# Two gate groups taken into an eighth set of block products, and a fixed pattern of partner steps

## The chip, the cores and the metric

The kernel runs on one NeuronCore of a Trainium2 chip. The metric is device time in microseconds (us) of one execution. Three runs of the kernel before gave 1090.18, 1089.87 and 1087.65 us, a median of 1089.87 us. The engines are named as in the profile: PE (TensorE, the matrix engine), PEld (its weight loads), DVE (VectorE), ACT (ScalarE), POOL (GpSimd) and SP (SyncE, which only issues transfers here).

## What is computed

One decoder layer on 256 tokens of width 2048. A single projection `h @ w_in` makes all inputs of two token mixers; each mixer is normed, gated by a SiLU, projected, and both are merged by sigmoid gates and projected out:

```python
proj = h @ w_in[l]
(a_q, a_k, a_v, a_g, a_lr, b_q, b_k, b_v, b_g, m_a, m_b) = jnp.split(proj, offsets, axis=-1)
...
o_a = rmsnorm(o_a, gla_norm_g[l]).reshape(B, S, GLA_VAL_DIM) * jax.nn.silu(a_g)
y_a = o_a @ w_branch_a[l]
...
o_b = o_b.reshape(B, S, DIFF_VAL_DIM) * jax.nn.silu(b_g)
y_b = o_b @ w_branch_b[l]
merged = jax.nn.sigmoid(m_a) * y_a + jax.nn.sigmoid(m_b) * y_b
out = merged @ w_out[l]
```

`o_a` is a gated linear attention (4 heads, called GLA below), `o_b` a differential attention (16 heads in four groups of four, each with queries `dq` and keys `dk`). Everything is in fp32. The columns of `a_g`, the gate of GLA, come in four groups of 512, called `ag0` to `ag3`; `m02`, `m03` are groups of `m_a`.

## The kernel before

**Three products for one.** A weight tile of 128 x 1024 numbers (a *half*) is loaded from HBM, rounded by ACT to a high part `hi` (L357), and the remainder `lo = w - hi` is made by DVE (L358). Each matmul product is then hi x hi, hi x lo, lo x hi, so a half is used by three matmuls per 128 x 512 block. `emit_half` prepares halves in the order of a list, `take` hands them to PE; `AHEAD` is 3, and there are three `hi` and three `lo` buffers, so preparation runs at most three halves ahead of PE.

**Plain products.** `token_major` computes a group of 512 columns for all 256 tokens in eight halves of 12 matmuls. `channel_major` (and `half_channel`, L552 is the shared `mm` helper) computes 128 columns with channels on partitions, two halves of 16 matmuls each: eight with 512 columns and eight with 256.

**Block products.** In the *phase*, sets of 1024 columns are computed by seven block products instead of eight (a fast 2 x 2 block scheme; `PRODUCTS` gives the order 1, 3, 5, 6, 2, 7, 4). Of the weight blocks the kernel needs sums, and builds them in two *chains* `a` and `b` (four buffers of 128 x 2048 in all, each chain in two parts t = 0 and 1):

- `link` loads a block into a chain; the POOL queue issues it (L227) once the buffer is free. The buffer of `a` part 0 of the next set is the one that product 7 part 0 frees; the last two are freed by product 4.
- After product 1 has been prepared, `follow_set` issues, for each half, a transfer that *accumulates* another block onto `a` (POOL queue, L251, 512 KB each, four per set). Product 5 reads the result.
- At steps (5,1), (6,0), (2,1) and (7,0) DVE adds `b` or the block `c` onto `a` (L260, two adds each); after the first two of these a block is accumulated onto `b` by a transfer, for product 7.

A *step* below is one slot (product, part): two halves of six matmuls. One set has 14 such slots. The last, smaller set (a *quarter* set, `SETS`) has only part 0 of each product: it gives the first half of the sum over channels for `ag3` and `m02`, whose other half is done plainly later.

**Partner steps.** Between slots, `phase_steps` puts halves of plain products (`v4`, GLA's keys and queries, `dq`/`dk` of the head groups in `EARLY`): the partners. Their weights are loaded by SP's queue (L308, 1 MB for the two halves of one channel tile, three `raw` buffers), so they need no chain. The phase's PE order is pinned as the list says.

Before, there are seven full sets, and each slot has one partner except 21 slots in `skip`: in sets 1 to 6 these are (4,0), (2,0) and (1,0), and (4,1) too in sets 5 and 6. So a set has 11 partners (10 at the end), 88 in all with four more at the start of set 0. The quarter set has six.

**After the phase** come `ag0` to `ag3` (`token_major`, then tanh on ACT and a gate on DVE, in `gate`), `m02`, the head group 3 (`diff_heads`), `m03`, and then the branch projections. Between their halves `pump` issues pieces of the GLA scores (exponentials, products and masks on ACT and DVE, small matmuls in `bg` banks), later GLA's output and the attention heads. Results of the phase wait in HBM (`spill`, POOL queue) and are fetched again.

Of the kernel before, what the change touches and what calls it, by code (L numbers as in the profile page):

```python
# [10 lines left out]
AF = mybir.ActivationFunctionType  # L11
# [3 lines left out]
P = 128  # L15
# [11 lines left out]
ROWS = {"two": 2, "tok": 4, "chan": KT}  # L27
WARM = 10
PRODUCTS = (1, 3, 5, 6, 2, 7, 4)
SETS = 7  # L30
QUARTER = ("ag3", "m02")
MERGE = (0, 1, 6)
LEAD = 6
EARLY = (0, 1, 2)
BIG = 18
MORE = 16
BRIDGE = 512
# [12 lines left out]
def chunk_plan():  # L50

    plan = [("v0", "two", "w_in", [(6144, RANK), (2048, 2 * VG[0] - RANK)])]
    at = 2 * VG[0] - RANK
    for g, n in enumerate(VG[2:]):
        plan.append((f"v{g + 2}", "tok", "w_in", [(2048 + at, n)]))
        at += n
    for hf in range(2):
        for name, base in (("k", 1024), ("q", 0)):
            for c in range(4):
                plan.append((f"{name}{hf}{c}", "chan", "w_in", [(base + 512 * hf + P * c, P)]))  # L60
    o = 6144 + RANK
    for s in range(2):
        plan.append((f"set{s}", "set", "w_in", [(o + 10240 + 1024 * s, 1024)]))
    for s in range(2, 6):
        plan.append((f"set{s}", "set", "w_in", [(o + base + 512 * (s - 2), 512) for base in (4096, 6144)]))
    plan.append(("set6", "set", "w_in", [(o + 8192, 1024)]))
    plan.append((f"set{SETS}", "quarter", "w_in", [(5632, 512), (o + 9216, 512)]))
    for g in range(4):
        plan.append((f"ag{g}", "rest" if g == 3 else "tok", "w_in", [(4096 + 512 * g, 512)]))
        for c in range(4):  # L70
            for n, name in enumerate(("dq", "dk")):
                plan.append((f"{name}{g}{c}", "chan", "w_in", [(o + 2048 * n + 512 * g + P * c, P)]))
        if g > 1:
            plan.append((f"m0{g}", "rest" if g == 2 else "tok", "w_in", [(o + 8192 + 512 * g, 512)]))
        for br in range(2):
            kind = "late" if br and g < 2 else "tok"
            plan.append((f"y{br}{g}", kind, ("w_branch_a", "w_branch_b")[br], [(512 * g, 512)]))
        plan.append((f"o{g}", "late", "w_out", [(512 * g, 512)]))
    plan.append(("ys0", "half", "w_branch_b", [(c, 512) for c in BRANCH_COLS]))
    for s, cols in enumerate(LATE_COLS):  # L80
        plan.append((f"os{s}", "half", "w_out", [(c, 512) for c in cols]))
    return plan
# [17 lines left out]
def phase_steps():  # L100

    keys = ["v4"] + [f"{name}{hf}{c}" for hf in range(2) for name in ("k", "q") for c in range(4)]
    keys += [f"{name}{g}{c}" for g in EARLY for pair in range(2) for name in ("dq", "dk") for c in (2 * pair, 2 * pair + 1)]
    other = [(key, r, h) for key in keys for r in range(4 if key == "v4" else 1) for h in range(2)]
    slots = [(s, prod, t) for s in range(SETS) for prod in PRODUCTS for t in range(2)]
    slots += [(SETS, prod, 0) for prod in PRODUCTS]
    front = [(0, prod, t) for prod in PRODUCTS[:2] for t in range(2)]
    skip = [(SETS, 4, 0), (SETS - 1, 4, 1), (SETS - 2, 4, 1)] + [(s, prod, 0) for prod in (4, 2, 1) for s in range(SETS - 1, 0, -1)]
    skip = skip[: len(slots) + len(front) - len(other)]
    mixed = []  # L110
    for slot in slots:
        mixed += [("set", *slot, h) for h in range(2)]
        for _ in range((slot not in skip) + (slot in front)):
            mixed.append(other.pop(0))
    return mixed + other

# [27 lines left out]
def hybrid_kernel(ctx: ExitStack, tc, xt, xn, preg, postg, w, w2, gkb, glag, lamv, diffg, ident_d, causal_d, lmask_d, out):  # L144
# [61 lines left out]
        return halves_of(*(f"{name}{g}{c}" for pair in range(2) for name in ("dq", "dk") for c in (2 * pair, 2 * pair + 1)))  # L206

    seq = halves_of("v0", "v2", "v3") + phase_steps()
    seq += halves_of(*(f"ag{g}" for g in range(4)))
    seq += halves_of("m02") + heads_order(3) + halves_of("m03", *(f"y0{g}" for g in range(4)))[:-4]  # L210
    seq += branch_steps() + late_steps() + halves_of("o2", "o3")
    ready = {}
    emitted = [0]
# [613 lines left out]
    def block_products(s):  # L827
        x = ps("mm")
        bank = {1: x, 6: x, 7: x, 4: x}
        kept, halves = {}, {}  # L830

        def right_done(b):
            dst = halves["r"][:, b, :]
            if s == SETS:
                return
            if s in MERGE:
                act.activation(dst, dst, AF.Tanh, scale=minus_half[:, b : b + 1])
            else:
                t = t2([P, 512], "tanh")
                act.activation(t, dst, AF.Tanh, scale=half_rstd[:, b : b + 1])  # L840
                dve.scalar_tensor_tensor(out=dst, in0=t, scalar=-1.0, in1=dst, op0=ALU.add, op1=ALU.mult)

        def left_done(b, src):
            if s in MERGE:
                act.activation(halves["l"][:, b, :], src, AF.Tanh, scale=half_rstd[:, b : b + 1])
            elif s < SETS:
                act.activation(halves["l"][:, b, :], src, AF.Copy, scale=rstd[:, b : b + 1])
            elif b:
                act.activation(halves["l"][:, b, :], src, AF.Copy)

        for prod in PRODUCTS:
            if prod not in bank:
                bank[prod] = ps("mm")
            out = bank[prod]
            few = 1 if s == SETS else 2
            for t in range(few):
                for h in range(2):
                    hi, lo = take(("set", s, prod, t, h))
                    for w, parts in ((hi, (0, 1)), (lo, (0,))):
                        for j in range(2):  # L860
                            kt = 4 * t + 2 * h + j
                            a = operand(prod, kt)
                            for part in parts:
                                first = prod not in (6, 7, 4) and kt == 0 and w is hi and part == 0
                                last = kt == 4 * few - 1 and w is lo
                                i = mm(out, a[part], w[:, 512 * j : 512 * j + 512], start=first, stop=last, skip_group_check=out is x)
                    latest[0] = i.ins
                    if t == few - 1 and h:
                        if prod in (1, 5):
                            kept[prod] = t2([P, 512], f"p{prod}")  # L870
                            act.activation(kept[prod], out, AF.Copy)
                        if prod == 5:
                            kept[3] = t2([P, 512], "p35")
                            dve.tensor_tensor(out=kept[3], in0=bank[3], in1=kept[5], op=ALU.add)
                        if prod == 6:
                            halves["r"] = u([P, 2, 512], "gr")
                            with tc.high_priority(offset=100):
                                dve.tensor_tensor(out=halves["r"][:, 0, :], in0=x, in1=kept[3], op=ALU.add)
                            right_done(0)
                        if prod == 2:  # L880
                            halves["l"] = u([P, 2, 512], "gl")
                            dve.tensor_tensor(out=halves["l"][:, 0, :], in0=out, in1=kept[1], op=ALU.add)
                            left_done(0, halves["l"][:, 0, :])
                        if prod == 7:
                            with tc.high_priority(offset=100):
                                dve.tensor_tensor(out=halves["r"][:, 1, :], in0=x, in1=kept[5], op=ALU.add)
                            right_done(1)
                            gspill[2 * s + 1] = spill(halves["r"], "gr")
                        if prod == 4:
                            left_done(1, x)  # L890
                            gspill[2 * s] = spill(halves["l"], "gl")
                    yield
# [376 lines left out]
    def other_parts(n):  # L1269
        return [fetch(gspill[n][:, b, :], "rest", lambda shape, name, dtype: t2(shape, name)) for b in range(2)]  # L1270

    for g in range(4):
        parts = other_parts(2 * SETS) if g == 3 else None
        banks = token_major(f"ag{g}", 512, x_ops, LANES)
        t = u2([P, 2, 512], "ua")
        for b in range(2):
            src = banks[b]
            if parts:
                src = parts[b]
                dve.tensor_tensor(out=src, in0=banks[b], in1=src, op=ALU.add)  # L1280
            gate(src, b, t[:, b, :])
        gates.append(t)
# [19 lines left out]
    m0.extend(gspill[12:14])  # L1302
    parts = other_parts(2 * SETS + 1)
    merge_gate(token_major("m02", 512, x_ops, LANES), parts)
    diff_heads(3)
    merge_gate(token_major("m03", 512, x_ops, LANES))

    while "out" not in done:
# [361 lines left out]
```

## Time and profile before

| | us |
|---|---|
| three runs | 1090.18, 1089.87, 1087.65 |
| median | 1089.87 |
| span of the profiled execution | 1087.3 |
| DVE busy in the span | 930.8 |
| ACT busy in the span | 720.0 |
| DMA traffic | 288.21 MB, mean 265 GB/s |

The span runs from the first to the last instruction of the profiled execution; the page gives no other time of that execution, and the median of the runs is 2.6 us above its span. "Busy" is the time in which an engine had an instruction under way, and a busy PE isn't one at its peak. DVE instructions follow each other before the one ahead has fully ended, so a run of them is read from start to start. A DMA row "to landing" is the time from issue to the last byte.

### The profile page before, as it was taken

What the parts mean: (1) busy time and instruction counts of PE and PEld (TensorE: products, weight loads), DVE (VectorE), ACT (ScalarE), POOL (GpSimd) and SP (SyncE); (2) the same over time, 40 slices, a digit from 0 to 9 for tenths busy, and PEclk for the clock granted to TensorE, in tenths of its full rate; (3) what the DMA queues carried; (4) which work ended last, traced back from release to release, by engine and by line L of the source; (5) the groups of instructions that cost most, each with busy time, mean ns of one, the idle gap of its engine ahead of it and who ended that gap; (6) DMA issues with size and microseconds to landing.
All of it is one profiled execution on the core that took longest, in us unless ns stands there. A gap on an engine that the chain in (4) does not pass through costs nothing.

```text
span 1087.3 us, 15367 instructions
## 1 busy us (share of the span) xinstructions
PE 1079.5 (99%) x5440; PEld 925.4 (85%) x5440; DVE 930.8 (86%) x1295; ACT 720.0 (66%) x1047; POOL 154.5 (14%) x229
## 2 busy tenths in 40 slices
PE   9999999999999999999999999999999999999997
PEld 8999888888888888888888888888888888888886
DVE  7787987979979899798998899877778878889886
ACT  7886766676766767667676465556777767566662
POOL 0201112121121211212102100021011011100000
PEclk9999999999999999999999999999999999999999
DMA  9889869799797997979968656599898898988752
GB/s 351 286 296 331 241 252 295 210 354 224 258 272 213 364 243 269 295 190 365 241 242 248 239 181 208 180 326 324 259 297 258 280 298 261 333 293 264 272 187 104
DMA packets 64941, 288.21 MB, mean 265 GB/s; under 512 B 8480, under 2 KB 11552, under 8 KB 46944
## 3 DMA queue, kind: packets, MB, share of 16 engines
q1 hardware_dynamic: 39520, 183.72, 48.2%
q0 software_dynamic: 24768, 102.77, 34.6%
q8 instruction: 43, 0.70, 0.3%
q10 hardware_dynamic: 576, 0.73, 0.2%
q14 instruction: 34, 0.28, 0.1%
HBM read 260.98 MB, written 26.21 MB: 264 GB/s over the span
## 4 chain that ended last, share of the span: by engine, by line
PE 88%; issue 5%; DMA 4%; DVE 2%; POOL 1%; ACT 0%; POOLq 0%; ACTq 0%; DVEq 0%
PE mm L552 54%; PE bg L552 24%; DMA a<-in_w_dram 2%; PE mm L540 2%; PE bg L540 2%; PE mm L525 1%; PE bg L977 1%; DVE lo L358 1%; DMA b<-in_w_dram 1%; PE bg L525 1%; DMA dl<-dk 1%; PE bg L1145 0%; PE bg L1119 0%; PE bg L444 0%; PE bg L1120 0%
## 5 line engine op out<-in xcount | busy, mean ns | idle before, releaser
L357 ACT ACTIVATE hi<-raw 128x1024 fp32r<-128x1024 f32 (+3 forms) x253 | 259.2, 1031 | 185.8 <-PE bg L552 89.9
L358 DVE TENSOR_TENSOR lo<-raw,hi 128x1024 fp32r<-128x1024 f32 (+3 forms) x255 | 300.3, 1183 | 63.9 <-ACT hi L357 59.3
L552 PE MATMUL mm<-hi,xs 128*128 128x512 f32 (+1 forms) x808 | 204.3, 386 | 0.0
L552 PEld LDWEIGHTS mm<-hi,xs 128*128 128x128 f32 x808 | 149.7, 188 | 25.0 <-ACT hi L357 0.2
L358 DVE TENSOR_TENSOR lo<-a,hi 128x1024 fp32r<-128x1024 f32 x120 | 144.7, 1220 | 23.7 <-ACT hi L357 22.9
L552 PE MATMUL bg<-xs,hi 128*128 128x512 f32 x640 | 164.9, 389 | 0.0
L357 ACT ACTIVATE hi<-a 128x1024 fp32r<-128x1024 f32 x120 | 127.0, 1060 | 47.2 <-PE mm L552 27.4
L552 PEld LDWEIGHTS bg<-xs,hi 128*128 128x128 f32 x640 | 120.3, 188 | 23.4
L552 PE MATMUL mm<-lo,xs 128*128 128x512 f32 (+1 forms) x404 | 113.1, 384 | 0.3 <-DVE lo L358 0.2
L552 PEld LDWEIGHTS bg<-xs,lo 128*128 128x128 f32 x640 | 87.2, 190 | 6.3
L552 PE MATMUL bg<-xs,lo 128*128 128x256 f32 x640 | 89.2, 282 | 0.0
L552 PEld LDWEIGHTS mm<-lo,xs 128*128 128x128 f32 x404 | 75.5, 188 | 14.6 <-DVE lo L358 1.1
L358 DVE TENSOR_TENSOR lo<-b,hi 128x1024 fp32r<-128x1024 f32 x60 | 72.4, 1221 | 6.5 <-ACT hi L357 5.0
L357 ACT ACTIVATE hi<-b 128x1024 fp32r<-128x1024 f32 x60 | 63.5, 1061 | 17.0 <-PE mm L552 14.7
L552 PE MATMUL mm<-hi,oah 128*128 128x512 f32 x128 | 50.8, 397 | 0.0
L552 PE MATMUL mm<-hi,oal 128*128 128x512 f32 x128 | 50.0, 391 | 0.0
L251 POOL DMA_DIRECT2D b<-in_w_dram x30 | 26.0, 869 | 138.5 <-DVE a L260 112.1
L1131 ACT ACTIVATE prob<-prob,mx,score_scale 128x128 f32<-128x128 f32 x64 | 34.3, 539 | 8.2 <-DVE mx L1126 8.0
L552 PE MATMUL mm<-hi,obh 128*128 128x512 f32 x96 | 37.7, 393 | 0.0
L552 PE MATMUL mm<-hi,obl 128*128 128x512 f32 x96 | 37.4, 390 | 0.0
L260 DVE TENSOR_TENSOR a<-a,b 128x1024 f32<-128x1024 f32 x30 | 36.3, 1221 | 0.3
L357 ACT ACTIVATE hi<-c 128x1024 fp32r<-128x1024 f32 x30 | 31.7, 1057 | 7.1 <-PE mm L552 4.9
(417 smaller groups left out, 2066.8 us busy)
## 6 DMA issues: line engine op xcount, KB each, us to landing
raw<-in_w_dram SPq DMA_DIRECT2D x110, 1024.0 KB, 6.8
a<-in_w_dram POOLq DMA_DIRECT2D x30, 512.0 KB, 12.6
c<-in_w_dram SPq DMA_DIRECT2D x30, 512.0 KB, 8.5
b<-in_w_dram POOLq DMA_DIRECT2D x30, 512.0 KB, 8.2
a<-in_w_dram POOLq DMA_DIRECT2D x13, 1024.0 KB, 8.5
b<-in_w_dram POOLq DMA_DIRECT2D x13, 1024.0 KB, 8.6
raw<-in_w_dram SPq DMA_DIRECT2D x14, 832.0 KB, 7.1
gr<-gr POOLq DMA_DIRECT2D x8, 512.0 KB, 7.9
```

The costliest lines, as they stand in the source:

```text
L251: pool.dma_start(chain[s, name, i][:, c], block(s, 1, i)[:, c], accum_op=ALU.add)
L260: dve.tensor_tensor(out=a, in0=a, in1=chain[s, "b", i][:, c] if second else raws[s, i, h], op=ALU.add)
L357: act.activation(hi_t[:, a:b], r[:, a:b], AF.Copy)
L358: dve.tensor_tensor(out=lo_t[:, a:b], in0=r[:, a:b], in1=f32(hi_t[:, a:b]), op=ALU.subtract)
L525: i = pe.matmul(out, lhs, rhs, start=first and n == 0, stop=last and n == len(pairs) - 1, **kw)
L540: i = pe.matmul(banks[g][b][:, :n], a[part][:, P * b : P * b + P], w[:, n * g : n * g + n], start=first, stop=last)
L552: i = pe.matmul(*args, **kw)
L977: pe.matmul(o, xk[:, P * c : P * c + P], xq.rearrange("p (b c t) -> p b c t", b=2, c=4)[:, :, c, :], start=i == 0, stop=i == 1)
L1131: act.activation(prob[m][:, lo:up], prob[m][:, lo:up], AF.Exp, scale=score_scale[:, b : b + 1], bias=mx[:, i : i + 1], accum_out=z[:, i : ...
```

## The change

The columns of `ag0` and `ag1` become an eighth full set (number 7, `GLA_GATES`), computed by block products in the phase. Its left and right halves get tanh and the SiLU form like the other gates, go to HBM with the other sets' results, and are fetched after the phase by two transfers in place of the two plain groups. The head group 2 leaves `EARLY`: its `dq` and `dk` are computed by `diff_heads` after `m02`, ahead of group 3's. The partners stand in a fixed pattern: in every full set behind (3,0), (5,1), (6,0), (6,1), (2,1), (7,0), (7,1) and (4,1), eight of 14 slots, and in the quarter set behind products 5, 6, 2 and 7. The four extra partners at the start of set 0 stay. That makes 72 partners.

```diff
-SETS = 7
+SETS = 8
+GLA_GATES = 7
...
-EARLY = (0, 1, 2)
+EARLY = (0, 1)
+PARTNERED = ((3, 0), (5, 1), (6, 0), (6, 1), (2, 1), (7, 0), (7, 1), (4, 1))
+LAST_PARTNERED = (5, 6, 2, 7)
...
+    plan.append((f"set{GLA_GATES}", "set", "w_in", [(4096, 1024)]))
     plan.append((f"set{SETS}", "quarter", "w_in", [(5632, 512), (o + 9216, 512)]))
     for g in range(4):
-        plan.append((f"ag{g}", "rest" if g == 3 else "tok", "w_in", [(4096 + 512 * g, 512)]))
+        if g > 1:
+            plan.append((f"ag{g}", "rest" if g == 3 else "tok", "w_in", [(4096 + 512 * g, 512)]))
...
-    skip = [(SETS, 4, 0), (SETS - 1, 4, 1), (SETS - 2, 4, 1)] + [(s, prod, 0) for prod in (4, 2, 1) for s in range(SETS - 1, 0, -1)]
-    skip = skip[: len(slots) + len(front) - len(other)]
     mixed = []
     for slot in slots:
         mixed += [("set", *slot, h) for h in range(2)]
-        for _ in range((slot not in skip) + (slot in front)):
+        s, prod, t = slot
+        with_partner = prod in LAST_PARTNERED if s == SETS else (prod, t) in PARTNERED
+        for _ in range(with_partner + (slot in front)):
             mixed.append(other.pop(0))
     return mixed + other
...
-    seq += halves_of(*(f"ag{g}" for g in range(4)))
-    seq += halves_of("m02") + heads_order(3) + halves_of("m03", *(f"y0{g}" for g in range(4)))[:-4]
+    seq += halves_of("ag2", "ag3", "m02") + heads_order(2) + heads_order(3) + halves_of("m03", *(f"y0{g}" for g in range(4)))[:-4]
...
+            elif s == GLA_GATES:
+                t = t2([P, 512], "tanh")
+                act.activation(t, src, AF.Tanh, scale=half_rstd[:, b : b + 1])
+                dve.scalar_tensor_tensor(out=halves["l"][:, b, :], in0=t, scalar=1.0, in1=src, op0=ALU.add, op1=ALU.mult)
...
-    for g in range(4):
+    for g in range(2):
+        gates.append(fetch(gspill[2 * GLA_GATES + g], "ua", u2))
+    for g in (2, 3):
         parts = other_parts(2 * SETS) if g == 3 else None
         banks = token_major(f"ag{g}", 512, x_ops, LANES)
...
-    diff_heads(3)
+    for g in (2, 3):
+        diff_heads(g)
     merge_gate(token_major("m03", 512, x_ops, LANES))
```

## The prediction

> **What bounds the kernel now.** I read the page first, then the busy time by windows, the chain of waits in order of time, and the DVE and POOL timelines of one set of the phase.
>
> ```profile
> PE 1079.5 (99%) x5440; PEld 925.4 (85%) x5440; DVE 930.8 (86%) x1295; ACT 720.0 (66%) x1047; POOL 154.5 (14%) x229
> PE 88%; issue 5%; DMA 4%; DVE 2%; POOL 1%; ACT 0%; POOLq 0%; ACTq 0%; DVEq 0%
> L357 ACT ACTIVATE hi<-a 128x1024 fp32r<-128x1024 f32 x120 | 127.0, 1060 | 47.2 <-PE mm L552 27.4
> ```
>
> PE is busy all the time, and the chain that ended last is 88% PE. Whether PE is at its full rate is seen in that chain in order of time (start, length, matmuls):
>
> ```profile
> 118.06 2.77 PE bg L552 x16
> ...
> 164.94 5.46 PE mm L552 x24
> ...
> 233.74 5.47 PE mm L552 x24
> ...
> 302.55 5.46 PE mm L552 x24
> ...
> 371.35 5.47 PE mm L552 x24
> ...
> 440.16 5.46 PE mm L552 x24
> ...
> 644.00 5.46 PE mm L552 x24
> ```
>
> 24 matmuls of 512 columns take 5.46 us, 0.2275 each, in the phase (the five rows from 164.94 to 440.16) and after it (the last row, two halves of `ag0`). A slot (12 matmuls) is so 2.75 us with its change-over, a partner half 2.77. Those five rows are also the starts of product 1 in sets 1 to 5; I call such a start X. From X to X: 68.8 us, and 14 slots with 11 partners sum to 14 x 2.75 + 11 x 2.77 = 69.0. **PE doesn't stall in the phase at all.** What it has behind it is less comfortable (PE, PEld, DVE, ACT, POOL busy, clock, DMA share, GB/s; the second window lies behind the phase):
>
> ```profile
> 300.30:369.20 68.90, 68.90 (x346) 58.67 (x345) 61.68 (x64) 47.05 (x55) 13.02 (x19) 1.00 0.88 276
> ...
> 640.00:690.00 50.00, 50.00 (x254) 42.57 (x253) 48.29 (x69) 27.21 (x36) 2.19 (x4) 1.00 0.60 204
> ```
>
> In a set DVE is busy 90% and the DMA engines 88%. Fewer partners shorten the set for PE by more than for these two.
>
> **The change part by part.**
>
> *Matmuls.* `ag0` and `ag1` are 16 halves of 12, 192 matmuls; the new set has 28 halves of 6, 168. 24 fewer, by the row at 644.00: **-5.5 us**. The head group 2 has the same matmuls wherever it stands: 0.
>
> *DVE in a set.* Starts in the DVE timeline give the pitch of back-to-back instructions:
>
> ```profile
> 317.42 1.23 DVE L358 TENSOR_TENSOR lo<-raw,hi 128x1024 fp32r<-128x1024 f32 x1 [1.99 <-ACT hi L357]
> ...
> 321.17 1.22 DVE L260 TENSOR_TENSOR a<-a,b 128x1024 f32<-128x1024 f32 x1
> 322.30 1.22 DVE L358 TENSOR_TENSOR lo<-raw,hi 128x1024 fp32r<-128x1024 f32 x1
> ...
> 333.45 0.69 DVE L874 TENSOR_TENSOR p<-mm,p 128x512 f32<-128x512 f32 x1
> 334.06 1.22 DVE L358 TENSOR_TENSOR lo<-raw,hi 128x1024 fp32r<-128x1024 f32 x1
> ...
> 364.31 1.23 DVE L358 TENSOR_TENSOR lo<-a,hi 128x1024 fp32r<-128x1024 f32 x1 [1.03 <-ACT hi L357]
> ```
>
> 1.13 us for 128x1024, 0.6 for 128x512. From 317.42 to 363.28 DVE has no gap. That is the heavy stretch, (5,1) to (4,0): 16 set halves and 6 partner halves (22 x 1.13), 8 adds (9.1), six evacuations (3.6) and some 2.4 for the partners' results make 40.0 us, against PE's 8 x 2.75 + 6 x 2.77 = 38.6. The new pattern has the same six partners here, so this stretch is unchanged: DVE enters with a lead of up to three halves and loses 1.4 us of it. In the other six slots the new set has 14 halves and one channel's result, 16.7 us of DVE in PE's 22.0. Over a new set that is 56.7 of 60.6 us, 94%. It fits, if nothing else takes the lead away first. Cost taken: 0; from the other side at most the whole 1.4 us in seven sets, 10.
>
> *The accumulating transfers.* This is where the pattern bites. The transfers onto `a` are issued when product 1 has been prepared, and product 5 reads them. Before, (3,0), (3,1) and (5,0) each had a partner and so had (1,1): (5,1) starts 24.8 us after X. Now only (3,0) has one: 5 x 2.75 + 2.77 = 16.5 us, and its second half at 17.9. By then `hi` must be made, which takes 1.06 (the L357 row), so the fourth transfer must have landed by **X + 16.8**. Issues of the fourth transfers of sets 1 to 5, and the landing times of each set's four (the largest is the fourth's):
>
> ```profile
> 169.06 0.84 POOL L251 DMA_DIRECT2D a<-in_w_dram  x1 [0.62 <-DVE lo L358]
> ...
> 237.31 0.86 POOL L251 DMA_DIRECT2D a<-in_w_dram  x1 [1.01 <-DVE lo L358]
> ...
> 305.93 0.88 POOL L178 DMA_DIRECT2D q<-q  x1
> 306.67 1.03 POOL L251 DMA_DIRECT2D a<-in_w_dram  x1
> ...
> 374.93 0.85 POOL L251 DMA_DIRECT2D a<-in_w_dram  x1 [1.02 <-DVE lo L358]
> ...
> 444.28 0.85 POOL L251 DMA_DIRECT2D a<-in_w_dram  x1 [0.61 <-DVE lo L358]
> ```
>
> ```profile
> DMA to landing us min/median/max: 9.9/13.9/18.6
> DMA to landing us min/median/max: 7.7/11.2/13.8
> DMA to landing us min/median/max: 9.9/11.7/16.3
> DMA to landing us min/median/max: 9.7/13.9/15.6
> DMA to landing us min/median/max: 11.6/14.5/17.1
> ```
>
> So they landed at X + 22.7, 17.4, 20.4, 19.2, 21.2: all in time for 24.8, all too late for 16.8, by 5.9, 0.6, 3.6, 2.4 and 4.4, mean 3.4. That is the upper price: 7 sets x 3.4 = 24 us. But part of these landings is the partners' own weights. DMA queues from the link of the last chain buffers (X - 8) to the landing, in sets 1 to 5 (packets, MB, share of the 16 engines; q1 is SP's queue), and in set 4 also POOL's:
>
> ```profile
> q1 hardware_dynamic: 863, 4.19, 35.9%
> q1 hardware_dynamic: 303, 2.21, 22.7%
> q1 hardware_dynamic: 300, 2.13, 17.9%
> q0 software_dynamic: 1507, 6.50, 78.9%
> q1 hardware_dynamic: 352, 2.62, 23.9%
> q1 hardware_dynamic: 327, 2.19, 18.1%
> ```
>
> In set 4 the shares add up to 103%: the engines are full, so what SP's queue moves is paid by the accumulates. Its 2.62 MB took 23.9% of 27.3 us, 6.5 us. In the new pattern one buffer of partner weights comes free in this window (behind (4,1); the next one behind (5,1)), so one transfer of 1.05 MB stays, 2.6 us, and 3.9 are freed: X + 15.3, in time. Likewise set 2 (5.8 us, 3.0 freed): 14.4, in time; set 3 (5.1, 2.6 freed, and the `q` spill ahead of the fourth transfer, 1.3 at this rate, isn't there any more): 16.5, in time; set 5 (5.3, 2.8 freed): 18.4, late by 1.6; set 1, where four loads of block `c` fall in and stay (11.1, 2.8 freed): 19.9, late by 3.1. I take set 1 once and the mean of the others, 0.4, for six sets: 3.1 + 2.4 = **+5.5 us**. Ends: 0 if POOL's order improves by a transfer, 24 if nothing is freed.
>
> That the engines are shared is also what the Trainium skill says (DMA: Bandwidth & Descriptors, section Issuing engines are not separate DMA queues): transfers started by different engines run on the same 16 DMA engines and interleave. With the rule the price is 5.5; without it 24.
>
> *The quarter set.* Its product 5 now follows two slots behind product 1, at X + 5.5 instead of two partners later. Before (first rows: the two issues; then PE at X):
>
> ```profile
> 572.07 0.90 POOL L251 DMA_DIRECT2D a<-in_w_dram  x1 [5.30 <-DVE lo L358]
> 573.20 0.88 POOL L251 DMA_DIRECT2D a<-in_w_dram  x1 [0.24 <-DVE lo L358]
> ```
>
> ```profile
> 572.05 1.07 PE L552 MATMUL mm<-hi,xs 128*128 128x512 f32 x4
> ```
>
> ```profile
> DMA to landing us min/median/max: 8.0/8.7/9.4
> DMA to landing us min/median/max: 5.7/8.2/12.0
> ```
>
> With a partner behind (4,1) they are issued at about X - 1.6 and X - 0.4, as set 4's. By the first landing row (these two) `hi` is ready at X + 7.5 and 10.1, needed at 5.5 and 6.9: 3.2 us. By the fastest of the second row (chain `b`, 5.7) it is nearly in time: 0. I take **+2 us**, nearer the row of the very place.
>
> *Behind the phase.* `dq`/`dk` of group 2 in place of `ag0`/`ag1`: as many halves, as many `pump` turns, the GLA work under the same 16 halves. DVE gets about 0.8 us of results per channel instead of 0.3 per two halves, eight times 0.5, in a stretch where it is busy 48.29 of 50; PE's cover are the later windows, where DVE rests. Taken 0, at most 4. POOL gets eight more spills between the GLA memsets and reads nothing for PE; the two fetched gates are needed only by GLA's output, behind all its scores. 0.
>
> *Sum.* -5.5 + 5.5 + 2 = +2. The span of the profiled execution would go from 1087.3 to 1089.3; the median lies 2.6 above the span, and the same is put on top: **1092 us**.
>
> **The rivals.** *All hidden*: the accumulates land in time everywhere and the quarter costs under 2 us. For it: the chain in the phase has no stall today, and in three of five sets the freed DMA time is enough. Against it: set 1 and the quarter. Time 1084.4 to 1086.4. *The accumulates stay where they were* (the slower side): landings depend on POOL's own chain of links and spills, not on SP's loads; PE waits at (5,1) in each set. It decides from a mean lateness of 1.1 us per set on (7 x 1.1 + 2 - 5.5 = 4.2). At 3.4 it is 1089.9 - 5.5 + 2 + 24 = 1110; half of that, 1098. For it: q0 alone holds 79% in set 4's window. *VectorE takes over*: a late `hi` at (5,1) empties the lead with which the heavy stretch is entered, and DVE's 1.4 us per set can't be caught up: 10 more than the sum, up to 1102. *The change gives nothing because DMA grows*: the new set moves 10.5 MB of blocks where `ag0` and `ag1` moved 8.4; that is the same wait again, priced above.
>
> **How the numbers follow.** A measurement of this kernel tells 0.3%, 3.3 us, from no change. Forecast (within 1086.6 to 1093.2): 0.35. All hidden: 0.27. Accumulates late by more than 1.1 us per set: 0.25; VectorE behind them: 0.13. So faster 0.27, same 0.35, slower 0.38. Range 1084.4 (nothing lost) to 1104, leaving the far end of the late case out.
>
> **What would show it.** After the change, from X to X: 60.6 us means no stall, 64 the late case. ACT's waits for `hi` on the DMA of `a` (before (5,1)) should be 0 to 3 us per set; DVE waiting for nothing from (5,1) to (4,0) with PE waiting for `lo` means the third rival. In the quarter set PE should stand about 2 us before product 5. The forecast is wrong if the DMA share falls in the light stretch, or if stalls appear behind the phase.

## The result and the profile after

The kernel after took 1121.62 us, the median of four runs (1120.19 to 1122.97). Four runs of the kernel before beside them gave 1088.89 (1087.65 to 1090.18). The ratio is 1.0296, with an interval of 1.0283 to 1.0309: **slower by 33 us**, where +2 was forecast, and beyond the upper end of the range. The span of the profiled execution grew from 1087.3 to 1119.2, by 31.9.

The page of the kernel after: span, busy time, chain by engine, and the group of `hi` made from `a` (its last two numbers are ACT's idle time ahead of it and what ended most of it):

```profile
span 1119.2 us, 15426 instructions
...
PE 1090.6 (97%) x5416; PEld 917.0 (82%) x5416; DVE 956.9 (85%) x1319; ACT 732.3 (65%) x1061; POOL 164.7 (15%) x245
...
PE 69%; DMA 13%; DVE 10%; issue 4%; ACT 2%; POOL 1%; DVEq 0%; POOLq 0%; ACTq 0%; SPq 0%
...
L361 ACT ACTIVATE hi<-a 128x1024 fp32r<-128x1024 f32 x136 | 143.9, 1058 | 86.0 <-DMA a<-in_w_dram 35.8
```

PE did the 24 matmuls less, and its share of the chain fell from 88% to 69%; DMA rose from 4% to 13% and DVE from 2% to 10%. ACT's idle time ahead of `hi<-a` grew from 47.2 to 86.0, and what ends it now is a transfer. PE's busy time doesn't tell this: it rose, although PE works less. (These lines stand four lower now: L251 is L255, L357 is L361, L552 is L556. In the experiments they shift by a few more, as each edit adds or takes lines.)

What waited inside the phase, by the waits from 80 to 640 us of the kernel after (us in total, times, longest):

```profile
ACT hi L361 <- DMA a<-in_w_dram: 35.8, 18, 2.7
PEld mm L556 <- ACT hi L361: 19.5, 16, 2.9
PE mm L556 <- ACT hi L361: 12.8, 13, 2.5
PEld bg L556 <- DVE lo L362: 12.4, 20, 1.0
PEld mm L556 <- DVE lo L362: 12.1, 27, 0.8
PE bg L556 <- DVE lo L362: 4.6, 12, 0.5
```

Two kinds of wait stand side by side: for `hi`, which waits for the accumulating transfer, and for `lo`, DVE's product. One set of the kernel after in ACT's timeline (start, length, idle before and its end); the first and the last row evacuate product 4 of two neighbouring sets, and from one to the other is what I call the *period*, here 64.74 us where PE needs 60.6:

```profile
212.32 0.67 ACT L849 ACTIVATE gl<-mm,half_rstd 128x512 f32<-128x512 f32 x1
...
227.31 1.06 ACT L361 ACTIVATE hi<-a 128x1024 fp32r<-128x1024 f32 x1 [1.08 <-DMA a<-in_w_dram]
...
231.08 1.06 ACT L361 ACTIVATE hi<-a 128x1024 fp32r<-128x1024 f32 x1 [2.70 <-DMA a<-in_w_dram]
...
233.53 1.06 ACT L361 ACTIVATE hi<-a 128x1024 fp32r<-128x1024 f32 x1 [1.40 <-DMA a<-in_w_dram]
...
277.06 0.67 ACT L855 ACTIVATE gl<-mm,rstd 128x512 f32<-128x512 f32 x1
```

ACT waits three times for transfers, 5.2 us in this set. PE, in its own timeline of the same set, takes the third and fourth `hi` (the rows at 231.08 and 233.53) the moment they are made, for (5,1):

```profile
230.94 0.61 PE L556 MATMUL mm<-lo,r1h 128*128 128x512 f32 x2
...
232.19 0.50 PE L556 MATMUL mm<-hi,r1h 128*128 128x512 f32 x1 [0.64 <-ACT hi L361]
...
234.65 0.50 PE L556 MATMUL mm<-hi,r1h 128*128 128x512 f32 x1 [0.46 <-ACT hi L361]
...
236.48 0.85 PE L556 MATMUL bg<-xs,hi 128*128 128x512 f32 x3
```

The first row is the last two matmuls of (5,0); two take 0.46, so (5,1) could have begun at 231.40 and begins 0.8 later. A half of six takes 1.36. The two halves are 2.46 apart, 1.1 more, and from the second one to the partner behind it (the last row) it is 1.83, another 0.5: (5,1) loses 2.4 in all. (X, the start of product 1, is 214.38 in this set.) The set lost 4.1. Read in the same way from PE's starts in all seven sets, some 31 us are lost: **18 in product 5, up to the end of (5,1), where PE waits for the late halves, and 12 behind it**, in the heavy stretch, which PE now enters with no half prepared ahead. (The rest is lost in products 1 and 3 of sets 1 and 2.)

With such periods the whole growth of the span can be placed (us; "needed" is the working of the prediction, 2.75 for a slot and 2.77 for a partner):

| part | before | after | needed | lost |
|---|---|---|---|---|
| end of set 0, six partners fewer | 162.7 | 147.3 | 146.1 | 1.2 |
| seven sets after it | | 65.0 64.7 65.1 65.1 65.9 64.2 65.0 | 60.6 each | 30.8 |
| quarter set, one partner fewer | 36.2 | 36.6 | 33.1 | 3.5 |
| behind it to the end of the span | 478.3 | 480.2 | 478.3 | 1.9 |

The quarter's period holds five partners now, four of its own and the one behind (4,1) of set 7. The losses sum to 37.4, less 5.5 for the matmuls: 31.9.

### The profile page after: what moved, and what is told of

It is laid out like the page before. It is cut to its first block, busy times and chain, and to the rows that moved or that the text cites. A ratio compares the mean times of both kernels' runs of the same rounds, so it can differ in the third digit from the quotient of the medians.

```text
span 1119.2 us, 15426 instructions
## 1 busy us (share of the span) xinstructions
PE 1090.6 (97%) x5416; PEld 917.0 (82%) x5416; DVE 956.9 (85%) x1319; ACT 732.3 (65%) x1061; POOL 164.7 (15%) x245
## 4 chain that ended last, share of the span: by engine, by line
PE 69%; DMA 13%; DVE 10%; issue 4%; ACT 2%; POOL 1%; DVEq 0%; POOLq 0%; ACTq 0%; SPq 0%
PE mm L556 43%; PE bg L556 16%; DMA a<-in_w_dram 9%; DVE lo L362 6%; DMA raw<-in_w_dram 3%; ACT hi L361 2%; DVE a L264 2%; PE mm L544 2%; PE bg L544 2%; PE mm L529 1%; PE bg L985 1%; DMA b<-in_w_dram 1%; PE bg L529 1%; DMA dl<-dk 1%; PE bg L1153 0%
## 5 line engine op out<-in xcount | busy, mean ns | idle before, releaser
L361 ACT ACTIVATE hi<-raw 128x1024 fp32r<-128x1024 f32 (+3 forms) x237 | 242.1, 1028 | 148.9 <-PE mm L556 68.8
L362 DVE TENSOR_TENSOR lo<-raw,hi 128x1024 fp32r<-128x1024 f32 (+3 forms) x239 | 281.9, 1185 | 38.2 <-ACT hi L361 35.3
L362 DVE TENSOR_TENSOR lo<-a,hi 128x1024 fp32r<-128x1024 f32 x136 | 165.6, 1221 | 53.0 <-ACT hi L361 50.8
L361 ACT ACTIVATE hi<-a 128x1024 fp32r<-128x1024 f32 x136 | 143.9, 1058 | 86.0 <-DMA a<-in_w_dram 35.8
L556 PE MATMUL mm<-hi,xs 128*128 128x512 f32 (+1 forms) x728 | 184.7, 384 | 0.0
L556 PEld LDWEIGHTS mm<-hi,xs 128*128 128x128 f32 x728 | 135.4, 188 | 22.2
L556 PE MATMUL bg<-xs,hi 128*128 128x512 f32 x512 | 132.2, 390 | 0.0
L556 PEld LDWEIGHTS bg<-xs,hi 128*128 128x128 f32 x512 | 96.4, 188 | 19.3
L556 PE MATMUL mm<-lo,xs 128*128 128x512 f32 (+1 forms) x364 | 104.2, 385 | 1.6 <-DVE lo L362 1.5
L361 ACT ACTIVATE hi<-b 128x1024 fp32r<-128x1024 f32 x68 | 71.4, 1059 | 26.3 <-PE mm L556 13.8
L556 PEld LDWEIGHTS bg<-xs,lo 128*128 128x128 f32 x512 | 68.3, 190 | 15.8 <-DVE lo L362 12.4
L556 PEld LDWEIGHTS mm<-lo,xs 128*128 128x128 f32 x364 | 67.4, 188 | 16.4 <-DVE lo L362 5.0
L556 PE MATMUL bg<-xs,lo 128*128 128x256 f32 x512 | 73.4, 286 | 4.6 <-DVE lo L362 4.6
L556 PE MATMUL mm<-xs,hi 128*128 128x512 f32 x256 | 68.0, 397 | 0.0
L255 POOL DMA_DIRECT2D b<-in_w_dram x34 | 29.2, 859 | 167.2 <-DVE a L264 115.7
L556 PEld LDWEIGHTS mm<-xs,hi 128*128 128x128 f32 x256 | 46.2, 189 | 7.8
L556 PE MATMUL mm<-hi,oah 128*128 128x512 f32 x128 | 50.8, 397 | 0.0
L556 PE MATMUL mm<-hi,oal 128*128 128x512 f32 x128 | 50.0, 391 | 0.0
L361 ACT ACTIVATE hi<-c 128x1024 fp32r<-128x1024 f32 x34 | 36.0, 1060 | 14.0 <-PE mm L556 10.7
L264 DVE TENSOR_TENSOR a<-a,c 128x1024 f32<-128x1024 f32 x34 | 41.3, 1219 | 0.0
```

Source lines behind the costliest of these rows:

```text
L255: pool.dma_start(chain[s, name, i][:, c], block(s, 1, i)[:, c], accum_op=ALU.add)
L264: dve.tensor_tensor(out=a, in0=a, in1=chain[s, "b", i][:, c] if second else raws[s, i, h], op=ALU.add)
L361: act.activation(hi_t[:, a:b], r[:, a:b], AF.Copy)
L362: dve.tensor_tensor(out=lo_t[:, a:b], in0=r[:, a:b], in1=f32(hi_t[:, a:b]), op=ALU.subtract)
L556: i = pe.matmul(*args, **kw)
```

## The experiments

Periods below are of sets 1 to 7, read as above. Single executions have no interval; the runs of before spread over 2.5 us, and differences below that aren't argued from the time but from periods and waits. All edits are made to the kernel after, but for one.

**The accumulating transfers taken away.**

```diff
-        if prod == 1:
-            accumulate("a", t)
```

> Changed kernel without the accumulating transfers onto chain a (that term is missing from products 5, 6 and 4). In the changed kernel a full set takes 65.0 us from set to set where its matmuls need 60.6. Theory L (late accumulates at (5,1) are the root, the later DVE waits follow from them): 60.6 to 61.5 us per set and some 3 us less in the quarter set, about 1090 us. Rival D (VectorE's heavy stretch costs by itself, about half of the 4.4 us): 62.8 us per set, about 1105 us.

Measured: 1092.18 us; periods 61.8 60.6 61.2 60.6 61.6 61.0 61.6, mean 61.2; quarter 33.5. Its waits from 80 to 640:

```profile
PEld mm L554 <- DVE lo L360: 5.7, 9, 2.5
PEld bg L554 <- DVE lo L360: 4.2, 6, 1.0
PE mm L554 <- DVE lo L360: 2.6, 3, 2.1
...
PEld mm L554 <- ACT hi L359: 1.1, 1, 1.1
```

The root is in these four transfers. Of 4.4 us per set 0.6 is left, and the waits for `lo` shrink along with those for `hi`: DVE keeps up when nothing empties its lead.

**The same traffic, without the wait.** Taking a transfer away takes its bytes away too. So each is turned into a plain copy into HBM.

```diff
         if prod == 1:
-            accumulate("a", t)
+            aside = dram.tile([P, 1024], F32, name=f"aside_{count[0]}")
+            pool.dma_start(aside, block(s, 1, t)[:, c])
```

> The kernel after, with the four transfers that accumulate onto chain a in every set turned into plain copies of the same block into a buffer in HBM that nobody reads: the same issues on POOL and the same bytes read, but product 5 waits for no transfer (it works without that block, so the output is another). If it is the wait of product 5 that costs: sets of 61.0 to 61.8, as where the transfers were left out, and 1091 to 1095 us. If the crowding of the DMA engines by these 2.1 MB costs by itself (links, partner weights and c late): sets of 62.5 and more, 1101 us and more.

Measured: 1118.88 us, with periods of 61.0 to 62.1 and set 0's end at 173.0. The design missed: nothing orders these copies, so they were moved to the start of the program:

```profile
1.91 4.26 POOL L259 DMA_DIRECT2D aside<-in_w_dram  x8
10.12 0.52 POOL L259 DMA_DIRECT2D aside<-in_w_dram  x1 [3.95 <-DMA aside<-in_w_dram]
```

There they hold up the first weights, 26 us by the end of set 0; in the sets the run only repeats the one before. It was made again with each copy kept at its place in POOL's order (`tc.keep_in_program_order`):

> As the run before it that copied the blocks aside, but each copy is kept at its place in POOL's order, behind the links of its set, so that its 512 KB pass through the DMA engines about when the accumulating transfer passed (a little sooner, for a copy waits for no buffer). Product 5 waits for no transfer and works without that block. If only the wait of product 5 costs: sets of 61.0 to 62, 1091 to 1096 us. If the crowding by these bytes costs by itself, through partner weights, c and links that land late: sets of 62.5 to 64.5, 1100 to 1115 us. Either way the bytes written to HBM grow by 17.8 MB, which the accumulates did not write.

Measured: 1093.56 us, periods 61.8 60.5 61.0 60.9 61.6 61.0 61.6. One set by windows (PE, PEld, DVE, ACT, POOL busy, clock, DMA share, GB/s): first the copies, then the transfers left out, then the kernel after:

```profile
332.60:393.50 60.90, 60.82 (x298) 51.05 (x297) 55.69 (x54) 42.06 (x48) 9.44 (x15) 1.00 0.86 283
```
```profile
330.50:391.10 60.60, 60.60 (x298) 51.03 (x297) 55.77 (x54) 42.22 (x47) 7.30 (x11) 1.00 0.77 249
```
```profile
212.30:277.10 64.80, 63.03 (x298) 50.48 (x297) 56.23 (x56) 41.69 (x48) 10.72 (x15) 1.00 0.83 258
```

With the copies the DMA engines are busier (0.86) and move more (283 GB/s) than in the kernel after, and PE hardly stalls (0.08 us of this set). **Busy DMA engines cost next to nothing here; product 5 waiting for the result of a transfer costs.** The crowding isn't quite the same: the copies wait for no buffer and go out 2 to 4 us sooner than the accumulates, and beside the second row they add 5.7 us of all engines to a set (0.86 x 60.9 less 0.77 x 60.6), the accumulates 7.1.

**The pattern without the eighth set.** The kernel *before*, with its 88 partners; only places move.

```diff
-    skip = [(SETS, 4, 0), (SETS - 1, 4, 1), (SETS - 2, 4, 1)] + [(s, prod, 0) for prod in (4, 2, 1) for s in range(SETS - 1, 0, -1)]
-    skip = skip[: len(slots) + len(front) - len(other)]
+    skip = [(SETS, 4, 0)] + [(s, *slot) for slot in ((1, 0), (1, 1), (3, 1), (5, 0)) for s in range(1, SETS)]
+    double = [(s, 4, 1) for s in range(1, SETS - 2)]
...
-        for _ in range((slot not in skip) + (slot in front)):
+        for _ in range((slot not in skip) + (slot in front) + (slot in double)):
```

> The kernel before, seven sets and 88 partners, all computation kept; only places of partners move: in sets 1 to 6 none behind (1,0), (1,1), (3,1) and (5,0), one behind (4,0) and (2,0), and two behind (4,1) in sets 1 to 4. So (5,1) starts 16.5 us after product 1, as in the kernel after, with everything else as before. My theory (the early (5,1) against accumulating transfers that land about X + 19): sets 1 to 6 grow from 68.8 (65.9 with ten partners) to 70.5 to 73.5, ACT waits for the DMA of a by some 2 us per set, and the time is 1101 to 1115; nearer the small end, since eight partners in the heavy stretch let DVE recover. Rival (the eighth set costs by its own DVE and DMA shares, and the late transfers only show it): sets stay within 0.5 us and the time is 1088 to 1092.

Measured: 1105.12 us; sets 1 to 6 by 72.5, 72.4, 69.0, 71.0, 69.2 and 66.8 (before: 68.8 five times and 65.9). Its waits from 160 to 590, and the same view of the kernel before from 80 to 640:

```profile
ACT hi L357 <- DMA a<-in_w_dram: 13.8, 7, 4.9
...
PE mm L552 <- ACT hi L357: 5.0, 4, 3.2
```
```profile
ACT hi L357 <- DMA a<-in_w_dram: 6.7, 4, 2.3
```

Half as much as the change costs, 16 us, comes with the pattern alone, 2 of it behind the phase. Set 1's period holds one partner less than before, so it lost more than its 72.5 shows. Counted from X to X, with the matmuls that each set holds, sets 1 to 6 lost 6.5, 3.6, 0.2, 1.6, 0.9 and 0.7 us. Their fourth transfers landed at X + 21.9, 18.8, 15.5, 16.5, 16.3 and 16.1, and PE needs them by X + 16.8 here too. So the two sets where they came 5.1 and 2.0 us late lost 1.3 and 1.8 us per us of lateness, most of it by the end of (5,1) (5.7 and 2.6): the heavy stretch has eight partners here, and DVE recovers soon. And three sets where they came 0.3 to 0.7 us ahead of that time still lost 0.7 to 1.6; only the one with 1.3 us to spare lost next to nothing.

**Partners spread over both sides of (5,1).**

```diff
-PARTNERED = ((3, 0), (5, 1), (6, 0), (6, 1), (2, 1), (7, 0), (7, 1), (4, 1))
+PARTNERED = ((1, 1), (3, 0), (3, 1), (5, 1), (6, 1), (2, 1), (7, 1), (4, 1))
```

> Partners behind (6,0) and (7,0) moved to (1,1) and (3,1), still eight per set: (5,1) starts 22.1 us after product 1 instead of 16.5, and the heavy stretch has four partners, PE 33.1 us against 36.9 of DVE. Theory L: the fourth accumulate (19 us after product 1) is in time, 61 to 62 us per set, about 1098 us. Rival D: 63 us or more per set with waits for lo in the heavy stretch, 1108 us or more.

Measured: 1110.21 us, periods 62.3 61.9 64.3 61.9 65.0 65.0 64.2, mean 63.5. From 80 to 640:

```profile
PEld mm L556 <- DVE lo L362: 27.5, 37, 1.6
PE mm L556 <- DVE lo L362: 14.2, 17, 1.2
ACT hi L361 <- DMA a<-in_w_dram: 12.7, 7, 2.7
```

The periods are above the 61 to 62 of theory L. One wait is traded for the other: two partners that moved ahead of (5,1) give the transfers time, and are missing in the heavy stretch, where PE now waits for `lo`.

**Block `c` loaded once.**

```diff
-            raws[s, i, j] = u([P, 1024], "c")
-            sp.dma_start(raws[s, i, j], block(s, 2, i)[:, 1024 * j : 1024 * j + 1024])
+            if s == 0:
+                raws[s, i, j] = u([P, 1024], "c")
+                sp.dma_start(raws[s, i, j], block(s, 2, i)[:, 1024 * j : 1024 * j + 1024])
+            else:
+                raws[s, i, j] = raws[0, i, j]
```

> Block c is loaded in set 0 and used again in the other full sets (their numbers are wrong there), 2.1 MB less per set, which in the changed kernel go out 15 us before product 1, among the links. Theory C (it is these loads that delay the accumulates, 2.1 MB at 2.4 us per MB): the fourth accumulate lands about 5 us earlier, 14 us after product 1, 60.6 to 61.5 us per set, about 1095 us. Rival (POOL's own chain of links and accumulates sets the landing): 64 to 65 us per set, about 1118 us.

Measured: 1111.28 us, periods 62.3 62.4 63.3 62.8 64.0 64.2 65.9, mean 63.6. From the first issue of four to the last landing it is 18.2 to 18.9 us in sets 1 to 5, where the kernel after has 20.6 to 21.1. So these loads hold the accumulates up there by some 2 us per set, not the 5 expected (in sets 6 and 7 by nothing: 19.7 and 20.8 us beside 19.8 and 19.9). The first issue lies 1.7 us before X: 18.5 is X + 16.8, just the deadline of the prediction. Sets 1 to 5 landed at X + 16.7 to 17.1 and still lose 1.7 to 3.4: 0.5 to 1.0 by the end of (5,1), the rest behind it. Landing in time for PE isn't enough.

**No DVE addition of `c` in the full sets.**

```diff
-            dve.tensor_tensor(out=a, in0=a, in1=chain[s, "b", i][:, c] if second else raws[s, i, h], op=ALU.add)
+            if second or s == SETS:
+                dve.tensor_tensor(out=a, in0=a, in1=chain[s, "b", i][:, c] if second else raws[s, i, h], op=ALU.add)
```

> Changed kernel without VectorE's four adds of c onto a in the full sets (that term is missing from product 4), 4.5 us of VectorE less behind (2,1) and (7,0). Transfers are the same, so the accumulates are as late. If the 4.4 us per set are direct lateness at (5,1) alone: 65 us per set, 1120 us. If about half of it is VectorE not catching up behind it: 62.5 to 63.5 us per set, about 1107 us.

Measured: 1104.59 us, periods 63.7 62.9 63.0 63.3 62.4 63.2 63.2, mean 63.1. ACT's wait for the transfers stays:

```profile
ACT hi L362 <- DMA a<-in_w_dram: 27.5, 15, 2.7
```

Of 4.4 us per set 1.9 go. Half of this is DVE making up for the lateness: behind (5,1) a set loses 0.7 where the kernel after loses 1.7 in the mean. The other half is won by the end of (5,1), since the fourth transfers land sooner here too, at X + 18.0 in the mean and X + 18.8 in the kernel after. So the expectation that the accumulates would be as late didn't quite hold, and this run doesn't separate the two causes cleanly.

**Ten partners, the head group 2 back in the phase.**

```diff
-EARLY = (0, 1)
-PARTNERED = ((3, 0), (5, 1), (6, 0), (6, 1), (2, 1), (7, 0), (7, 1), (4, 1))
+EARLY = (0, 1, 2)
+PARTNERED = ((1, 1), (3, 0), (3, 1), (5, 1), (6, 0), (6, 1), (2, 1), (7, 0), (7, 1), (4, 1))
...
-    seq += halves_of("ag2", "ag3", "m02") + heads_order(2) + heads_order(3) + ...
+    seq += halves_of("ag2", "ag3", "m02") + heads_order(3) + ...
```

> Eight sets with the head group 2 back in the phase: ten partners per full set, the two more behind (1,1) and (3,1). Theory L: no late accumulates, 66.1 us per set as its matmuls need, so that the phase has no stall; rival D says the same, since the heavy stretch is the one of the kernel before. Behind the phase 16 halves less lie over the GLA work: if they were its cover, PE waits there, up to 30 us; if not, the total is about 1085 us.

Measured: 1129.38 us; periods 66.2 67.8 71.2 68.8 67.4 66.7 68.2, mean 68.0 where PE needs 66.2 and both theories had 66.1. Landing is 22.6 to 28.4 us after the first issue: partner weights take the time that the partners give. And behind the phase the span shrank by 17.5 us only (480.2 to 462.7), while a head group is 16 halves of 2.77, some 44 us of matmuls. There, PE in 900 to 950 us of this kernel:

```profile
900.00:950.00 50.00, 39.99 (x191) 33.36 (x190) 32.97 (x89) 27.29 (x69) 6.14 (x8) 0.90 0.80 246
```

PE stands 10 of 50 us there and is granted 0.90 of its clock; in the kernel after, the five windows of 50 us from 790 to 1040 hold 0.2 us of idle PE. The head group behind the phase was cover, and it costs more to take it away than the ten partners give.

**Product 2 ahead of product 5.** That puts two slots more between products 1 and 5, without a partner more.

```diff
-PRODUCTS = (1, 3, 5, 6, 2, 7, 4)
+PRODUCTS = (1, 3, 2, 5, 6, 7, 4)
...
-LEAD = 6
+LEAD = 4
...
-PARTNERED = ((3, 0), (5, 1), (6, 0), (6, 1), (2, 1), (7, 0), (7, 1), (4, 1))
-LAST_PARTNERED = (5, 6, 2, 7)
+PARTNERED = ((2, 0), (5, 1), (6, 0), (6, 1), (7, 0), (7, 1), (4, 0), (4, 1))
+LAST_PARTNERED = (3, 2, 6, 7)
...
-        steps = {(5, 0): 0, (2, 0): 0} if s == SETS else {(5, 1): 0, (6, 0): 1, (2, 1): 0, (7, 0): 1}
+        steps = {(5, 0): 0, (7, 0): 0} if s == SETS else {(5, 1): 0, (6, 0): 1, (7, 0): 0, (7, 1): 1}
```

> Changed kernel with product 2 ahead of 5 (order 1, 3, 2, 5, 6, 7, 4; the adds of c onto a move to (7,0) and (7,1)) and the partners behind (2,0), (5,1), (6,0), (6,1), (7,0), (7,1), (4,0), (4,1); in the quarter set behind 3, 2, 6, 7. No weight or matmul more or less, (5,1) starts 22.0 us after product 1. Theory L (the late accumulates, and the lead of VectorE that they use up): 61 to 62.5 us per set and 2 us less in the quarter set, 1092 to 1100 us. Rival D (heavy stretch itself: here 33.3 us of VectorE in 30.4 of PE from (5,1) to (7,1)): 64 us or more per set, 1112 us or more.

Measured: 1110.81 us, ratio 1.0199 (1.0169 to 1.0228); periods 61.5 61.4 62.5 62.4 62.7 62.1 63.3, mean 62.3: 19 of the 31 us come back, at the same matmuls and bytes. Theory L's period held, its total didn't: 9 are given away elsewhere: set 0 ends 6.7 later, since product 2 needs sums there that aren't made yet, and the quarter takes 2.0 more. The same with one partner of the heavy stretch, (7,0), moved ahead of it, to (1,1):

> As the run before, but the partner of (7,0) stands behind (1,1): (5,1) starts 24.8 us after product 1, as in the kernel before, and the heavy stretch has one partner less. Theory L: no wait for the accumulates any more; if VectorE keeps up 61 us per set, about 1090 us. Rival D: waits for lo from (6,0) on, 63 to 65 us per set, 1105 us or more.

Measured: 1128.99 us, ratio 1.0366 (1.0336 to 1.0396); mean period 64.5. From 80 to 640:

```profile
PEld mm L556 <- DVE lo L362: 20.2, 28, 1.4
PEld bg L556 <- DVE lo L362: 15.3, 17, 1.0
...
PE mm L556 <- DVE lo L362: 9.6, 18, 0.9
PE bg L556 <- DVE lo L362: 8.4, 16, 0.6
```

ACT waits for no transfer onto `a` any more, and for those onto `b` less than in the run before (8.8 us, 12.0), but one partner misplaced costs 2.2 us in each set: here PE waits for DVE.

**The quarter set.**

```diff
-LAST_PARTNERED = (5, 6, 2, 7)
+LAST_PARTNERED = (1, 3, 6, 7)
```

> Changed kernel, only the quarter set's partners moved from products 5, 6, 2, 7 to 1, 3, 6, 7: product 5 starts 11 us after product 1 instead of 5.5. Both theories: the full sets stay at 65.0 us. The quarter set loses its wait of some 3 us: about 1118 us; if that wait isn't from the accumulates, no change, 1121 us.

Measured: 1118.47 us; the quarter takes 33.9 instead of 36.6, the other periods are as after. PE's waits in the quarter (602 to 645 us), in the kernel after and here:

```profile
PE mm L556 <- ACT hi L361: 2.5, 1, 2.5
```
```profile
PE mm L556 <- DVE lo L362: 0.5, 1, 0.5
```

**The best pieces together.** Set 0 as in the kernel after, product 2 early in sets 1 to 7, and this quarter.

```diff
+TWO_FIRST = (1, 3, 2, 5, 6, 7, 4)
+TWO_PARTNERED = ((2, 0), (5, 1), (6, 0), (6, 1), (7, 0), (7, 1), (4, 0), (4, 1))
+def order_of(s):
+    return PRODUCTS if s in (0, SETS) else TWO_FIRST
```

> The kernel after, all computation kept, with the three best pieces seen so far together: set 0 in the order and with the partners of after (it ended at 147.3), sets 1 to 7 with product 2 ahead of product 5 and two partners moved behind it (62.3 each), the quarter set with partners behind products 1, 3, 6 and 7 (33.9). If the pieces add up: 147.3 + 7 x 62.3 + 33.9 + 480 = 1097 for the span and 1099 to 1100 us, still slower than the kernel before. If what the order gains is given back at its borders (the sums for product 2 in set 0, the loads of c): 1105 us and more. Faster than before would need sets at 60.6 with no wait at all.

Measured: 1100.70 us, ratio 1.0108 (1.0076 to 1.0141), 21 us below the kernel after and 12 above before. Set 0 ends at 147.2, the periods are 63.5 61.3 62.4 61.9 62.7 62.1 63.3, the quarter takes 33.9: the pieces add up. What is left in the phase (80 to 640) is DVE, and late landings of `b` in sets 1, 3 and 6:

```profile
PEld mm L563 <- DVE lo L369: 11.4, 17, 1.6
PEld bg L563 <- DVE lo L369: 9.1, 18, 1.0
ACT hi L368 <- DMA b<-in_w_dram: 6.9, 4, 2.6
PE mm L563 <- DVE lo L369: 5.2, 7, 1.2
```

No version with the eighth set came below the kernel before. All that it could win is the 5.5 us of matmuls, and even with the transfers left out sets keep 0.6 each.

## Why the prediction was wrong, by its steps

**Matmuls, -5.5: held.** Without the transfers' wait the kernel takes 1092.2 and 1093.6 us, and their losses (7 x 0.6 in the sets, 0.9 in set 0, 0.4 in the quarter, 3.4 behind the phase) less 5.5 make 3.4, where the first one's span exceeds that of before by 3.1.

**The accumulating transfers, +5.5: the sets lost 30.8, with what the transfers set off in DVE, and 26.7 of it goes when they are left out. This is the step that failed**, in three places.

*"One transfer of 1.05 MB stays, 2.6 us, and 3.9 are freed"* fell. The transfers from X - 8.2 to the last landing in the kernel after (206.2 to 233.5): the engines' busy tenths and the GB/s in 40 slices, the queues, and the landing time of the links of `b`:

```profile
DMA  9999998999999999999999999999999999999999
GB/s 444 426 420 384 384 270 264 396 432 426 426 438 474 384 420 456 444 408 396 444 444 342 234 198 222 216 216 204 228 360 366 282 204 198 216 216 234 192 198 210
...
q0 software_dynamic: 1353, 6.51, 80.7%
q1 hardware_dynamic: 530, 2.43, 22.9%
...
b<-in_w_dram POOLq DMA_DIRECT2D x2, 1024.0 KB, 11.9
```

SP's queue moves nearly what it moved in set 4 of before (2.62 MB, 23.9%). I had counted which partner weights come free; I hadn't counted what else stands in SP's order; the loads of `c` I had counted in set 1 alone. SP's timeline ahead of this set, and ahead of set 4 of the kernel before:

```profile
199.32 0.33 SPq L312 DMA_DIRECT2D raw<-in_w_dram  x1
199.69 2.57 SPq L247 DMA_DIRECT2D c<-in_w_dram  x4
210.99 0.33 SPq L312 DMA_DIRECT2D raw<-in_w_dram  x1
```
```profile
348.95 2.08 SPq L243 DMA_DIRECT2D c<-in_w_dram  x4
```

The four loads of `c`, 2.1 MB, stand behind a load of partner weights that waits for its buffer. They went out 14.7 us before X, and 22.4 before it (371.35) in the kernel before. So they move beside the links, which take 11.9 us to land (9.1 in set 4 of before), and the accumulates come behind those. The run with `c` loaded once puts this at 2 us of landing. The last of the four issues of this set, and the landing times of the four (the largest is its own):

```profile
218.66 0.85 POOL L255 DMA_DIRECT2D a<-in_w_dram  x1 [0.60 <-DVE lo L362]
```
```profile
DMA to landing us min/median/max: 12.1/13.5/14.8
```

218.66 + 14.8 is X + 19.1, in the midst of the five landings of before (X + 17.4 to 22.7), not the X + 14.4 to 16.5 that I had for most sets. The rule of the Trainium skill that I set beside it (DMA: Bandwidth & Descriptors, section Issuing engines are not separate DMA queues) agrees with this trace: the two shares add up to 104%, the engines are full and shared. What was wrong is how much SP's queue would move.

*"The fourth transfer must have landed by X + 16.8"* was the wrong deadline. It is the moment at which PE needs the half; but preparation runs up to three halves ahead of PE, and this lead has to be there when the heavy stretch begins. With `c` loaded once the landings of sets 1 to 5 met the deadline within 0.3 us, and the sets still lost 1.7 to 3.4 us. In the kernel before with the pattern moved, landings 0.3 to 0.7 us ahead of the deadline cost 0.7 to 1.6, and one 1.3 us ahead cost 0.2. That what is missing is the lead fits both; no run changed the lead alone.

*"7 sets x 3.4 = 24 us"* was no upper price. It charged a us of lateness with a us. The fourth transfers of the seven sets landed at X + 18.0 to 19.4, 2.0 us late in the mean, less than the 3.4 charged, and the sets lost 4.4 each, 3.8 of it by the transfers: about 1.9 us per us. In the set shown 2.4 us were lost at (5,1), 0.5 in product 3 ahead of it and 1.3 behind it, where DVE has 40.0 us of work for PE's 38.6 and can't catch up. Relieved of four additions, DVE left 0.7 per set behind (5,1) in place of 1.7; with eight partners in the heavy stretch of the kernel before, a us of lateness cost 1.3 and 1.8.

**DVE in a set, 0: held by itself, not together with the lateness.** Where nothing is late, sets lose 0.6 (4 in seven sets, of the 10 allowed). The rivals stood as alternatives, "the accumulates stay where they were" to 1110 and "VectorE takes over" to 1102; they happened together, the second set off by the first. Their prices, 24 and 10, add up to 34 beside the 30.8 measured, but that is luck: the lateness was smaller than the one priced, and each us of it cost more. I had named this chain in the third rival, a late `hi` that empties the lead, and then hung its price on the forecast's sum instead of on the second rival's.

**The quarter, +2: measured 3.5** beside the working, 3.2 beside the kernel before, whose quarter was itself 0.3 above it. That is the far end that I had named, 3.2. The mechanism was right: one wait for `hi` of 2.5 us, which goes when the partners stand ahead of product 5.

**Behind the phase, 0: measured 1.9**, within 4. PE waits 0.8 us more for `lo` there. The remaining 1.1 wasn't settled, nor why this part took 3.4 longer than before with the transfers left out. That the head group is cover there was shown by taking it away.

The signs named in the prediction told the case: "64 the late case" for X to X (65.0), ACT waiting for the DMA of `a` (5.2 us in the set shown, where 0 to 3 was named), and PE's waits for `lo` beside it.

## What to carry to other kernels

Before work between an issue and its use is taken out, list all that stands in *each* queue of that window, and what each entry waits for: a load behind one that waits for a buffer moves with it. A transfer's deadline is not when the slowest engine needs the data. It lies earlier (here a set with 1.3 us to spare lost 0.2, one with 0.7 to spare lost 0.7), by what seems to be the lead with which the next dense stretch has to be entered; and where that stretch is as full as here (40.0 us of DVE for 38.6 of PE), price a us of lateness at up to two. Two rivals that feed each other need a row for both together.

## What the runs showed of the hardware

Accumulating transfers kept the DMA engines busy about twice as long as plain ones. In the window from 206.2 to 233.5 shown above the engines are full throughout, at some 380 to 475 GB/s in most of the first half and at 190 to 235 in most of the last third, where the accumulates run. POOL's queue by itself shows it in two stretches: from 205.0 to 227.3 of the run with the copies in place it moves plain transfers only, and from 228.6 to 233.5 of the kernel after accumulates only:

```profile
q0 software_dynamic: 1291, 6.25, 67.9%
```
```profile
q0 software_dynamic: 279, 1.01, 105.5%
```

The first is 15.1 us of all engines for 6.25 MB, 2.4 us per MB. The second is 5.2 us for 1.01 MB, 5.1 per MB; a share above 100% shows that the edges of such a window count, so these are estimates. In the window from X - 8.2 to the last landing POOL's queue took 80.7% of 27.3 us, 22.0 us. Alone it would so have landed the fourth transfer near X + 14 at best, had SP moved nothing: the pattern left about 3 us between that and the deadline, before any lead.
